# Seven-product feed-forwards of a two-layer decoder trunk: partial sums accumulated in PSUM instead of added by VectorE

## The chip, the cores and the metric

The kernel runs on one core of a Trainium2 chip. The metric is device time in microseconds, the median of several runs of the whole program. A profile of one further execution gives what each engine did and when.

## What is computed

Two layers, each a token mixer and a gated feed-forward with a convolution, every one of them between two RMS norms, on 512 tokens of 1024 features in float32. Layer 0 mixes with dilated attention, layer 1 with a gated linear recurrence. The change lies in the feed-forward of both layers:

```python
def conv_ffn(x, w_up, conv_w, conv_b, w_down):
    u = causal_dwconv(x @ w_up, conv_w, conv_b)
    g, v = u[..., :D_FF], u[..., D_FF:]
    return (jax.nn.gelu(g, approximate=True) * v) @ w_down
```

`w_up` is 1024 x 6144, `w_down` 3072 x 1024. The same seven-product scheme also serves the values of attention, where the change only turns signs.

## The kernel before, in words

**Precision.** Every operand is split into a high part `hi` (fp32r) and a rest `lo`. A product is three TensorE passes, hi·hi, hi·lo and lo·hi (`PASSES`). ScalarE makes `hi` (line 253, `whi` for weights), VectorE makes `lo` as the difference (line 265, `wlo`). Weights arrive as `raw` tiles over the Sync queue, or as `sum` tiles: one block is loaded and another added to it by a GpSimd DMA that accumulates. Up to eight split weight units are alive at once (`W_UNITS`), and `tick()`, called after every tile of the program, splits the next ones.

**Feature tiles.** The usual tile of the up projection (`feat`, line 570) is 24 matmuls of 512 columns into one PSUM bank `ps`. Then ScalarE applies the middle tap of the convolution and the bias (line 817), VectorE adds two more taps (line 821), both reading the bank, and gelu (line 831) and the gate product (line 833) follow.

**Seven products for eight.** Some pairs of blocks are multiplied as 2 x 2 block matrices with seven products instead of eight. The tokens' four corners enter directly or as *token sums* (T1 to T4, `token_sums`, line 583: VectorE adds at line 608, ScalarE takes `hi` at line 610, VectorE `lo` at line 614); the weights' sums come through the DMAs. In the *up* projection this is `sevenths` (line 840): seven products of 24 matmuls with 256 columns, for two of the six groups in `PAIRS`. Each yields one bank `vq`. Its steps are woven between feature tiles by `WIDE_STEPS = (1, 3, 1, 2)`: one product after the first tile, three after the second, one after the third, two after the fourth. In the *down* projection it is `down_unit` (line 967), two units in each feed-forward, each with seven products of 24 matmuls with 512 columns into two banks. `DOWN_AT` places each product behind a feature tile.

**What becomes of a product.** ScalarE copies the first results to SBUF (`y` and `c`, lines 869 and 872; `c` at line 990), VectorE adds or subtracts every further product from its bank (lines 873 to 887 and, through `each`, 647) and writes the outputs (`w` at line 864; `o`, `y`, `c`). Every product takes new banks from the pool of eight, oldest free one first.

**Order.** The schedule is manual: on each engine instructions run as the program wrote them. ScalarE's row for a product therefore stands behind everything that was written before it, whether that waits or not. The token sums of a feed-forward are made while its first feature tiles run, one step per `tick`.

Of the kernel before, what the change touches and what calls it, by code (L numbers as in the profile page):

```python
# [18 lines left out]
P = 128  # L19
# [76 lines left out]
def kernel(  # L96
# [485 lines left out]

    def token_sums(hT):

        made = {}
        terms_of = {
            3: [((1, 1), 1), ((0, 1), -1)],
            2: [((0, 0), 1)],
            4: [((1, 0), -1)],
            1: [((0, 1), 1), ((0, 0), -1)],  # L590
        }

        def make(pace):
            pace = iter(pace)
            prior, rest = None, []
            for name in (3, 2, 4, 1):
                hi, lo = (htp.tile([P, 4, 256], F32R, tag="x", name=nm("T"), bufs=8) for _ in range(2))
                made[name] = hi, lo
                parts = [(corner(hT, *ij)(x).bitcast(F32), sg) for ij, sg in terms_of[name] for x in range(2)]
                if name in (3, 1):  # L600
                    first = parts.pop(0)[0]
                    prior = [first[:, 2 * h : 2 * h + 2] for h in range(2)]
                r = [gen(s="run").rearrange("p (k c) -> p k c", k=2) for _ in range(2)]
                for h in range(2):
                    k = slice(2 * h, 2 * h + 2)
                    a = prior[h]
                    for b, sg in parts:
                        nc.vector.tensor_tensor(r[h], a, b[:, k], op=ALU.add if sg > 0 else ALU.subtract)  # L608
                        a = r[h]
                    nc.scalar.activation(hi[:, k], r[h], AF.Copy)  # L610
                    for f in rest:
                        f()
                    rest = [
                        lambda k=k, a=a, hi=hi, lo=lo: nc.vector.tensor_tensor(
                            lo[:, k], a, hi[:, k].bitcast(F32), op=ALU.subtract
                        )
                    ]
# [6 lines left out]
    def product(banks, act):  # L624
        i = chunk()
        while plan[i][0] == "first":
            i = chunk()
        for j in range(2):
            W = take(i, j)
            for u in range(2):  # L630
                for k in range(2):
                    for n, (a, b) in enumerate(PASSES):
                        mm(  # L633
                            banks[u],
                            act(a)[:, 2 * j + k, u * P : (u + 1) * P],
                            woven(W[b][:, k, :]),
                            start=(j, k, n) == (0, 0, 0),
                            stop=(j, k, n) == (1, 1, 2),
                        )
            done()  # L640
# [4 lines left out]
    def each(dst, a, b, op):  # L645
        for u in range(2):
            nc.vector.tensor_tensor(dst[u], a[u], b[u], op=op)

# [163 lines left out]
    def ffn(layer, hT, post, pre, spill):  # L812
# [27 lines left out]
        def sevenths(j, n):  # L840
            outs = {}

            def product(piece, act, *then):
                W = take(*piece)
                q = psum("vq")
                for n in range(2):
                    for k in range(4):
                        mm3(
                            q[:, n * 256 : (n + 1) * 256],
                            [w[:, k, n * P : (n + 1) * P] for w in W],  # L850
                            [woven(act(a)[:, k, :]) for a in range(2)],
                            k == 0,
                            k == 3,
                        )
                done()
                return q

            def out(p, s, a, q, op):
                if p not in outs:
                    outs[p] = [gen(s="w") for _ in range(2)]  # L860
                for n in range(2):
                    c = slice(n * 256, (n + 1) * 256)
                    dst = outs[p][n].rearrange("p (a b s) -> p s a b", a=2, s=2)[:, s]
                    nc.vector.tensor_tensor(dst, unwoven(a[:, c]), unwoven(q[:, c]), op=op)
# [7 lines left out]
            nc.scalar.activation(c, q, AF.Copy)  # L872
# [27 lines left out]
        def operands(base):  # L900
# [9 lines left out]
            def of(src, sign=None, prior=None):  # L910
                hi, lo = slot(), slot()
                whole = sign is not None
                if whole:
# [5 lines left out]
                    nc.scalar.activation(hi, run, AF.Copy)  # L919
# [4 lines left out]
                if whole:  # L924
                    nc.vector.tensor_tensor(lo, run, hi.bitcast(F32), op=ALU.subtract)
# [8 lines left out]
            yield of(piece(0, 0), 1)  # L934
            yield of(piece(1, 0), -1)
            yield of(piece(1, 1))
            yield of(piece(0, 0), -1, piece(0, 1))
# [29 lines left out]
        def down_unit(unit, ops):  # L967

            c, y = [gen(s="c") for _ in range(2)], [gen(s="y") for _ in range(2)]

            def step(combine):
                op = ready.pop(0)
                q = two()
                product(q, lambda a: op[a])
                begin_operand(ops)
                write()
                combine(q)
# [10 lines left out]
            def p1(q):  # L988
                for u in range(2):
                    nc.scalar.activation(c[u], q[u], AF.Copy)  # L990

            def p2(q):
                each(y, c, q, ALU.add)

            def p3(q):
                o = [gen(s="o") for _ in range(2)]
                each(o, c, q, ALU.add)
                out(0, 0, o)

            def p4(q):  # L1000
                each(y, q, y, ALU.subtract)
                each(c, q, c, ALU.subtract)

            def p5(q):
                o = [gen(s="o") for _ in range(2)]
                each(o, y, q, ALU.subtract)
                out(1, 0, o)

            def p6(q):
                each(c, q, c, ALU.subtract)  # L1010

            def p7(q):
                each(y, y, q, ALU.add)
                each(c, c, q, ALU.subtract)
                out(1, 1, y)
                out(0, 1, c)

            for p in (p1, p2, p3, p4, p5, p6, p7):
                step(p)
# [58 lines left out]
    def attention(hT, post, pre, spill):  # L1078
# [129 lines left out]
        def value_steps(out, c=None):  # L1208
# [20 lines left out]
            each(y, q, y, ALU.subtract)  # L1229
            each(c, q, c, ALU.subtract)  # L1230
# [3 lines left out]
            each(c, q, c, ALU.subtract)  # L1234
# [4 lines left out]
            each(o, y, q, ALU.subtract)  # L1239
# [4 lines left out]
            each(y, y, q, ALU.add)  # L1244
            each(c, c, q, ALU.subtract)
# [615 lines left out]
```

## Time and profile before

| | |
|---|---|
| median of 3 runs | 1375.66 us (1374.78 to 1377.14) |
| the profiled execution | 1376.62 us |
| its span, first to last instruction | 1374.9 us |
| TensorE busy | 1354.0 us, 98% |
| VectorE busy | 1052.6 us, 77% |
| ScalarE busy | 671.5 us, 49% |
| mean granted TensorE clock | 0.997 |

The engines are called PE (TensorE matmul), PEld (its weight load), DVE (VectorE), ACT (ScalarE), POOL (GpSimd) and SP (SyncE) in the profile. Rows of a timeline give start, duration, engine, line, operation, output<-input and shape; "[3.65 <-DVE run L608]" is the idle time of the engine before that row and what ended it. Matmuls are pipelined, so that the duration of one is more than the distance from one start to the next: the distance is what a matmul costs. The first feed-forward runs from about 485 to 850 us, the second from about 1003 us to the end.

### The profile page before, as it was taken

What the parts mean: (1) busy time and instruction counts of PE and PEld (TensorE: products, weight loads), DVE (VectorE), ACT (ScalarE), POOL (GpSimd) and SP (SyncE); (2) the same over time, 40 slices, a digit from 0 to 9 for tenths busy, and PEclk for the clock granted to TensorE, in tenths of its full rate; (3) what the DMA queues carried; (4) which work ended last, traced back from release to release, by engine and by line L of the source; (5) the groups of instructions that cost most, each with busy time, mean ns of one, the idle gap of its engine ahead of it and who ended that gap; (6) DMA issues with size and microseconds to landing.
All of it is one profiled execution on the core that took longest, in us unless ns stands there. A gap on an engine that the chain in (4) does not pass through costs nothing.

```text
span 1374.9 us, 18692 instructions
## 1 busy us (share of the span) xinstructions
PE 1354.0 (98%) x7109; PEld 1199.2 (87%) x7109; DVE 1052.6 (77%) x1838; ACT 671.5 (49%) x1125; POOL 111.3 (8%) x126
## 2 busy tenths in 40 slices
PE   9999999999999999999999999999999999999997
PEld 6888888888888889998888889888899998888886
DVE  7786573737676778887958789878978888968785
ACT  5434432414355554455535445579653455545452
POOL 1211021011000001000001020000001000000020
PEclk9999999999999999999999999999999999999999
DMA  8979779695749354465757784233153665768771
GB/s 256 246 218 281 193 189 250 204 215 160 254 141 307 108 154 114 147 184 122 198 155 199 214 240 159 92 123 122 62 153 105 158 165 133 191 169 213 212 201 62
DMA packets 184238, 243.11 MB, mean 177 GB/s; under 512 B 16633, under 2 KB 135937, under 8 KB 184147
## 3 DMA queue, kind: packets, MB, share of 16 engines
q1 hardware_dynamic: 151456, 184.82, 41.0%
q0 software_dynamic: 32688, 57.09, 21.5%
q8 instruction: 56, 0.92, 0.3%
q14 instruction: 36, 0.29, 0.1%
q10 hardware_dynamic: 2, 0.00, 0.0%
HBM read 218.23 MB, written 28.36 MB: 179 GB/s over the span
## 4 chain that ended last, share of the span: by engine, by line
PE 46%; DVE 32%; ACT 11%; DMA 7%; issue 3%; DVEq 0%; SPq 0%; ACTq 0%; POOLq 0%
PE ps L436 24%; PE vq L633 10%; DVE wlo L265 9%; DVE u L821 8%; PE acc L436 7%; DMA sum<-in_ffn_w_down_dram 3%; ACT whi L253 3%; ACT u L817 2%; DVE run L608 2%; DMA raw<-in_ffn_w_down_dram 1%; DVE u L833 1%; ACT u L831 1%; DVE xb L1580 1%; PE O L1465 1%; PE S L1386 1%
## 5 line engine op out<-in xcount | busy, mean ns | idle before, releaser
L436 PE MATMUL ps<-hT,whi 128*128 128x512 f32 (+1 forms) x2528 | 698.4, 362 | 0.8 <-DVE hT L499 0.6
L436 PEld LDWEIGHTS ps<-hT,whi 128*128 128x128 f32 x2528 | 459.9, 190 | 57.5 <-ACT whi L253 1.3
L436 PE MATMUL ps<-hT,wlo 128*128 128x512 f32 (+1 forms) x1264 | 456.4, 361 | 0.2 <-DVE wlo L265 0.2
L265 DVE TENSOR_TENSOR wlo<-raw,whi 128x1024 fp32r<-128x1024 f32 x233 | 280.1, 1217 | 21.7 <-ACT whi L253 21.7
L253 ACT ACTIVATE whi<-raw 128x1024 fp32r<-128x1024 f32 x233 | 239.0, 1051 | 112.9 <-DMA raw<-in_attn_w_qkv_dram 77.1
L436 PEld LDWEIGHTS ps<-hT,wlo 128*128 128x128 f32 x1264 | 240.1, 190 | 28.5 <-DVE wlo L265 0.6
L821 DVE SCALAR_TENSOR_TENSOR u<-ps,cols,u 128x511 f32<-128x511 f32 (+1 forms) x160 | 119.5, 747 | 73.5 <-ACT u L817 70.6
L253 ACT ACTIVATE whi<-sum 128x1024 fp32r<-128x1024 f32 x68 | 70.8, 1051 | 137.6 <-DMA sum<-in_attn_w_qkv_dram 71.7
L633 PE MATMUL vq<-whi,A 128*128 128x512 f32 x448 | 137.8, 379 | 0.0
L265 DVE TENSOR_TENSOR wlo<-sum,whi 128x1024 fp32r<-128x1024 f32 x68 | 82.0, 1217 | 54.2 <-ACT whi L253 54.2
L436 PE MATMUL acc<-whi,alo 128*128 128x512 f32 x256 | 97.3, 380 | 1.2 <-DVE alo L185 1.2
L436 PE MATMUL acc<-whi,ahi 128*128 128x512 f32 x256 | 98.2, 383 | 0.0
L436 PE MATMUL acc<-wlo,ahi 128*128 128x512 f32 x256 | 97.1, 379 | 0.2 <-DVE wlo L265 0.2
L633 PEld LDWEIGHTS vq<-whi,A 128*128 128x128 f32 x448 | 84.7, 189 | 12.0
L633 PE MATMUL vq<-wlo,A 128*128 128x512 f32 x224 | 85.1, 380 | 2.0 <-DVE wlo L265 2.0
L831 ACT ACTIVATE u<-u 128x512 f32<-128x512 f32 x48 | 30.3, 631 | 111.2 <-DVE u L821 111.2
L817 ACT ACTIVATE u<-ps,cols 128x512 f32<-128x512 f32 x80 | 61.0, 763 | 6.6 <-PE ps L436 6.6
L633 PE MATMUL vq<-whi,T 128*128 128x512 f32 x192 | 59.7, 382 | 0.0
L436 PEld LDWEIGHTS acc<-whi,alo 128*128 128x128 f32 x256 | 48.4, 189 | 9.1 <-DVE alo L185 2.4
L436 PEld LDWEIGHTS acc<-wlo,ahi 128*128 128x128 f32 x256 | 48.4, 189 | 7.1 <-DVE wlo L265 0.6
L436 PEld LDWEIGHTS acc<-whi,ahi 128*128 128x128 f32 x256 | 48.4, 189 | 6.6 <-ACT ahi L184 0.2
L633 PEld LDWEIGHTS vq<-wlo,A 128*128 128x128 f32 x224 | 42.3, 189 | 8.8 <-DVE wlo L265 2.9
(245 smaller groups left out, 1778.9 us busy)
## 6 DMA issues: line engine op xcount, KB each, us to landing
raw<-in_ffn_w_up_dram SPq DMA_DIRECT2D x44, 1024.0 KB
raw<-in_attn_w_qkv_dram SPq DMA_DIRECT2D x25, 1024.0 KB
raw<-in_ffn_w_down_dram SPq DMA_DIRECT2D x16, 1024.0 KB
sum<-in_ffn_w_down_dram POOLq DMA_DIRECT2D x16, 1024.0 KB, 8.7
sum<-in_attn_w_qkv_dram POOLq DMA_DIRECT2D x24, 512.0 KB, 8.1
raw<-in_attn_w_qkv_dram SPq DMA_DIRECT2D x16, 512.0 KB
sum<-in_ffn_w_down_dram SPq DMA_DIRECT2D x8, 1024.0 KB
raw<-in_lru_w_in_dram SPq DMA_DIRECT2D x8, 1024.0 KB
```

The source lines that it names most:

```text
L253: nc.scalar.activation(hi, raw, AF.Copy)
L265: nc.vector.tensor_tensor(lo, raw, hi.bitcast(F32), op=ALU.subtract)
L436: mm(dst, l[a], r[b], start=start and n == 0, stop=stop and n == 2)
L608: nc.vector.tensor_tensor(r[h], a, b[:, k], op=ALU.add if sg > 0 else ALU.subtract)
L633: mm(banks[u], act(a)[:, 2 * j + k, u * P : (u + 1) * P], woven(W[b][:, k, :]), start=(j, k, n) == (0, 0, 0), stop=(j, k, n) == (1, 1, 2),)
L817: nc.scalar.activation(u, ps, AF.Identity, scale=cc[:, j : j + 1], bias=cc[:, 48 + j : 49 + j])
L821: nc.vector.scalar_tensor_tensor(u[:, d:], ps[:, : S - d], wc, u[:, d:], op0=ALU.mult, op1=ALU.add)
L831: nc.scalar.activation(u, u, AF.Gelu_apprx_tanh)
L833: nc.vector.tensor_tensor(gv[k], gv[k], u, op=ALU.mult)
L1386: mm(ps[:, c], q[hh][:, c], keys, start=True, stop=True)
L1465: mm(po[:, c], vtile(v, r, 2 * gi + hh), pts[gi][:, r], start=gi == 0, stop=gi == 1)
L1580: nc.vector.scalar_tensor_tensor(u[:, d:], ps[:, : S - d], wc, u[:, d:], op0=ALU.mult, op1=ALU.add)
```

## The change

**Accumulation.** `product` takes a flag `first`; without it the first matmul does not clear the bank, and the product adds to what lies there. In each set of seven two chains run so: products 1 and 5 in bank W, and products 2, 4 and 7 (down) or 2, 4 and 6 (up) in bank X. The remaining ones go to a bank of their own (Z). So that all additions have the right sign, token sums 1 and 2 are negated (`flip`: ScalarE copies with scale −1, VectorE makes `lo` by one scalar_tensor_tensor).

**Copies.** `kept` has ScalarE copy a partial sum out of its bank in the middle of a chain. VectorE then adds once for each output.

**Signs elsewhere.** Attention's value steps use the same token sums; additions become subtractions, and twelve tensor_tensor operations become scalar_tensor_tensor (`less`).

The core of the diff:

```diff
+    def low(lo, whole, hi, flip=False):
+        if flip:
+            nc.vector.scalar_tensor_tensor(lo, whole, -1.0, hi.bitcast(F32), op0=ALU.mult, op1=ALU.subtract)
+        else:
+            nc.vector.tensor_tensor(lo, whole, hi.bitcast(F32), op=ALU.subtract)
+
+    def kept(bank, scale=1.0):
+        t = gen(s="c")
+        nc.scalar.activation(t, bank, AF.Copy, scale=scale)
+        return t
...
-            1: [((0, 1), 1), ((0, 0), -1)],
+            1: [((0, 0), 1), ((0, 1), -1)],
...
-                    nc.scalar.activation(hi[:, k], r[h], AF.Copy)
+                    nc.scalar.activation(hi[:, k], r[h], AF.Copy, scale=-1.0 if name == 2 else 1.0)
...
-            tt, add, sub = nc.vector.tensor_tensor, ALU.add, ALU.subtract
-            c, y = gen(s="c"), gen(s="y")
-            q = product((n + 5, 0), total_of(3))
-            nc.scalar.activation(y, q, AF.Copy)
+            add, sub = ALU.add, ALU.subtract
+            W, X = psum("W"), psum("X")
+            product(W, (n + 5, 0), total_of(3))
+            w = kept(W, -1.0)
             yield
-            q = product((n + 4, 0), corner(hT, 0, 0))
-            nc.scalar.activation(c, q, AF.Copy)
-            tt(y, y, q, op=add)
+            product(X, (n + 4, 0), corner(hT, 0, 0))
+            c = kept(X)
             yield
-            q = product((n + 4, 1), corner(hT, 1, 0))
-            out(0, 0, c, q, add)
+            Z = psum("Z")
+            product(Z, (n + 4, 1), corner(hT, 1, 0))
+            out(0, 0, c, Z, add)
             yield
-            q = product((n + 5, 1), total_of(2))
-            tt(y, q, y, op=sub)
-            tt(c, q, c, op=sub)
+            product(X, (n + 5, 1), total_of(2), False)
+            u = kept(X, -1.0)
             yield
-            q = product((n + 7, 0), total_of(4))
-            out(1, 0, y, q, sub)
+            product(W, (n + 7, 0), total_of(4), False)
+            out(1, 0, u, W, sub)
             yield
-            q = product((n + 7, 1), total_of(1))
-            out(1, 1, y, q, add)
-            tt(c, c, q, op=add)
+            product(X, (n + 7, 1), total_of(1), False)
+            out(0, 1, X)
+            out(1, 1, w, X, sub)
             yield
-            q = product((n + 8, 0), corner(hT, 1, 1))
-            out(0, 1, q, c, sub)
+            Z = psum("Z")
+            product(Z, (n + 8, 0), corner(hT, 1, 1))
+            out(0, 1, None, Z, add)
...
-            for p in (p1, p2, p3, p4, p5, p6, p7):
-                step(p)
+            def last(q):
+                o = [kept(b) for b in q]
+                made(1, 1, "w", ALU.subtract)(q)
+                each(o, o, held.pop("z"), ALU.add)
+                out(0, 1, o)
+
+            for do in (
+                (X, True, keep("c")),
+                (W, True, keep("w", -1.0)),
+                (None, True, made(0, 0, "c", ALU.add)),
+                (X, False, keep("u", -1.0)),
+                (W, False, made(1, 0, "u", ALU.subtract)),
+                (None, True, keep("z")),
+                (X, False, last),
+            ):
+                step(*do)
                 yield
```

In `down_unit`, `keep` copies both banks of a product with `kept`, and `made` lets VectorE combine a held copy with the banks into an output.

What stands where now: TensorE in the first set of `sevenths` of the first feed-forward, before. These are the first matmuls of the second product (`vq987`), the last of the third (`vq991`) and the first of the fourth (`vq996`):

```order
L436 MATMUL vq987_5067<-hT0780_3932,whi945_4814 128x256
L436 MATMUL vq987_5067<-hT1781_3933,whi945_4814 128x256
...
L436 MATMUL vq991_5105<-hT1781_3933,whi950_4855 128x256
L436 MATMUL vq991_5105<-hT0780_3932,wlo951_4856 128x256
L436 MATMUL vq996_5140<-T954_4889,whi958_4897 128x256
L436 MATMUL vq996_5140<-T955_4890,whi958_4897 128x256
```

And the same place after the change:

```order
L860 MATMUL X974_4988<-hT0780_3932,whi945_4814 128x256
L860 MATMUL X974_4988<-hT1781_3933,whi945_4814 128x256
...
L860 MATMUL Z991_5104<-hT1781_3933,whi950_4855 128x256
L860 MATMUL Z991_5104<-hT0780_3932,wlo951_4856 128x256
L860 MATMUL X974_4988<-T954_4889,whi958_4897 128x256
L860 MATMUL X974_4988<-T955_4890,whi958_4897 128x256
```

The matmuls stand in the same order; the second and the fourth product now write one bank, X, with only the third between them.

ScalarE at that place, before (`T` are token sums, `whi` weights, `u` a feature tile's convolution, `c` the copy of the second product):

```order
L817 ACTIVATE u979_5048<-ps978_5023,cols366_1819 128x512
L610 ACTIVATE T980_5052<-run982_5054 128x512
L253 ACTIVATE whi984_5061<-raw960_4901 128x1024
L872 ACTIVATE c973_4987<-vq987_5067 128x512
L610 ACTIVATE T980_5052<-run983_5055 128x512
L253 ACTIVATE whi988_5099<-sum920_4603 128x1024
L253 ACTIVATE whi994_5135<-raw986_5065 128x1024
L253 ACTIVATE whi997_5169<-sum920_4603 128x1024
```

And after:

```order
L829 ACTIVATE u979_5048<-ps978_5023,cols366_1819 128x512
L621 ACTIVATE T980_5052<-run982_5054 128x512
L253 ACTIVATE whi984_5061<-raw960_4901 128x1024
L591 ACTIVATE c987_5091<-X974_4988 128x512
L621 ACTIVATE T980_5052<-run983_5055 128x512
L253 ACTIVATE whi988_5098<-sum920_4603 128x1024
L253 ACTIVATE whi994_5134<-raw986_5065 128x1024
L591 ACTIVATE c996_5163<-X974_4988 128x512
L253 ACTIVATE whi997_5167<-sum920_4603 128x1024
```

The copy of the second product keeps its place; a copy of X after the fourth product (`c996`) is new, ahead of a weight split.

More of the change, by code (lines that the diff above doesn't have):

```diff
@@ L622, in token_sums, with product @@
         return (lambda name: lambda a: made[name][a]), make
-    def product(banks, act):
+    def product(banks, act, first=True):
         i = chunk()
@@ L636, in product @@
                             woven(W[b][:, k, :]),
-                            start=(j, k, n) == (0, 0, 0),
+                            start=first and (j, k, n) == (0, 0, 0),
                             stop=(j, k, n) == (1, 1, 2),
+                            skip_group_check=True,
                         )
@@ L647, in each, with less @@
             nc.vector.tensor_tensor(dst[u], a[u], b[u], op=op)
+    def less(dst, a, b):
+        for u in range(2):
+            nc.vector.scalar_tensor_tensor(dst[u], a[u], -1.0, b[u], op0=ALU.mult, op1=ALU.subtract)
     def feat_tiles(n, hT, sink, halves=False, between=None, at=None, paired=True):
@@ L841, in sevenths, with product, out @@
             outs = {}
-            def product(piece, act, *then):
+            def product(bank, piece, act, first=True):
                 W = take(*piece)
-                q = psum("vq")
                 for n in range(2):
                     for k in range(4):
[L848 to L854, printed above, removed]
+                        for p, (a, b) in enumerate(PASSES):
+                            mm(
+                                bank[:, n * 256 : (n + 1) * 256],
+                                W[a][:, k, n * P : (n + 1) * P],
+                                woven(act(b)[:, k, :]),
+                                start=first and (n, k, p) == (0, 0, 0),
+                                stop=(k, p) == (3, 2),
+                                skip_group_check=True,
+                            )
                 done()
-                return q
-            def out(p, s, a, q, op):
+            def out(p, s, a, q=None, op=None):
                 if p not in outs:
@@ L908, in operands, with of @@
             run = slot(F32)
-            def of(src, sign=None, prior=None):
+            def of(src, sign=None, prior=None, flip=False):
                 hi, lo = slot(), slot()
@@ L924, in of @@
                 if whole:
-                    nc.vector.tensor_tensor(lo, run, hi.bitcast(F32), op=ALU.subtract)
+                    low(lo, run, hi, flip)
                 else:
@@ L967, in down_unit, with step @@
         def down_unit(unit, ops):
-            c, y = [gen(s="c") for _ in range(2)], [gen(s="y") for _ in range(2)]
-            def step(combine):
+            W, X, held = two("W"), two("X"), {}
+            def step(banks, first, then):
                 op = ready.pop(0)
-                q = two()
-                product(q, lambda a: op[a])
+                q = banks or two()
+                product(q, lambda a: op[a], first)
                 begin_operand(ops)
                 write()
-                combine(q)
+                then(q)
                 end_operand()
@@ L986, in out, with keep, f, made @@
                         parts[t, p] = tiles[u]
[L988 to L1016, printed above, removed]
-            for p in (p1, p2, p3, p4, p5, p6, p7):
-                step(p)
+            def keep(name, scale=1.0):
+                def f(q):
+                    held[name] = [kept(b, scale) for b in q]
+                return f
+            def made(p, s, name, op):
+                def f(q):
+                    o = held.pop(name)
+                    each(o, o, q, op)
+                    out(p, s, o)
+                return f
+            def last(q):
[13 more added lines that the diff above has]
+                step(*do)
                 yield
@@ L1228, in value_steps @@
             product(q, total_of(2))
-            each(y, q, y, ALU.subtract)
-            each(c, q, c, ALU.subtract)
+            each(y, q, y, ALU.add)
+            each(c, q, c, ALU.add)
             yield
@@ L1233, in value_steps @@
             product(q, corner(hT, 1, 1))
-            each(c, q, c, ALU.subtract)
+            each(c, q, c, ALU.add)
             yield
@@ L1238, in value_steps @@
             o = [gen(s="v") for _ in range(2)]
-            each(o, y, q, ALU.subtract)
+            less(o, y, q)
             out(1, 0, o)
@@ L1243, in value_steps @@
             product(q, total_of(1))
-            each(y, y, q, ALU.add)
-            each(c, c, q, ALU.subtract)
+            less(y, y, q)
+            each(c, c, q, ALU.add)
             out(1, 1, y)
```

17 lines of the change are left out of this document (8 added, 9 removed).

## The prediction

> **What bounds the kernel now.** I read the page first, then TensorE's waits, then the order of time on TensorE and ScalarE around the seven products.
>
> ```profile
> PE 1354.0 (98%) x7109; PEld 1199.2 (87%) x7109; DVE 1052.6 (77%) x1838; ACT 671.5 (49%) x1125; POOL 111.3 (8%) x126
> PE 46%; DVE 32%; ACT 11%; DMA 7%; issue 3%; DVEq 0%; SPq 0%; ACTq 0%; POOLq 0%
> ```
>
> TensorE is busy for 1354.0 of 1374.9 us, and the change leaves it every matmul. VectorE work that is removed can therefore give back only what TensorE waits for, at most the 20.9 us in which it is idle. The second line, the chain, still runs over VectorE for 32%: in the feed-forwards TensorE runs ahead of VectorE and ScalarE, and the chain follows the laggards until TensorE once meets them. The waits say how often it does:
>
> ```profile
> PE tr L489 <- DVE xs L481: 4.0, 3, 2.6
> PE vq L633 <- DVE wlo L265: 2.0, 2, 1.2
> PE acc L436 <- DVE alo L185: 1.2, 1, 1.2
> ```
>
> The first line is the norm between two layers, which the change does not touch. The other two, 3.2 us together, lie in feed-forwards and hang on VectorE being late. They are what a lighter VectorE can win. The first of them stands behind a transfer:
>
> ```profile
> 682.75 6.65 DMA sum<-in_ffn_w_down_dram
> 690.04 12.83 DMA sum<-in_ffn_w_down_dram
> ```
>
> VectorE's splits free the sum tile at 682.7, two transfers follow, and the weights reach TensorE too late.
>
> **The new wait.** In `sevenths` (one set of seven products of the up projection, 24 matmuls of 256 columns each) the second product now goes to bank X, the third to Z, and the fourth into X again. ScalarE's copy `c` reads X after the second product, so the fourth must wait for that copy. Before, the fourth had a bank of its own. Here are the first matmuls of products two, three and four of the first set in the first feed-forward, and then ScalarE's rows up to the copy:
>
> ```profile
> 541.56 0.38 PE L436 MATMUL vq<-hT,whi 128*128 128x256 f32 x2
> ...
> 544.24 0.39 PE L436 MATMUL vq<-hT,whi 128*128 128x256 f32 x2
> ...
> 546.92 0.39 PE L436 MATMUL vq<-T,whi 128*128 128x256 f32 x2
> ```
>
> ```profile
> 553.05 0.63 ACT L610 ACTIVATE T<-run 128x512 fp32r<-128x512 f32 x1 [3.65 <-DVE run L608]
> 553.59 1.05 ACT L253 ACTIVATE whi<-raw 128x1024 fp32r<-128x1024 f32 x1
> 554.54 0.58 ACT L872 ACTIVATE c<-vq 128x512 f32<-128x512 f32 x1
> ```
>
> The second product ends as the third begins, near 544.2; the copy runs from 554.54 to 555.12, over 10 us later, because ScalarE works through a token sum (which waited for VectorE) and a weight split first. Up to this point the order shows the same instructions on both engines as before, but for the sign in two splits. So the copy comes no earlier, and the fourth product, which started at 546.92, cannot start before 555.12: 8.20 us of TensorE standing still. The second feed-forward repeats it:
>
> ```profile
> 1066.45 0.39 PE L436 MATMUL vq<-T,whi 128*128 128x256 f32 x2
> ```
>
> ```profile
> 1074.07 0.58 ACT L872 ACTIVATE c<-vq 128x512 f32<-128x512 f32 x1
> ```
>
> 1074.65 − 1066.45 is again 8.20 us. To each I add 0.05 for the handing on and 0.13 for two splits of the token sums, which lie on the chain ahead of the copy and become scalar_tensor_tensor (priced below): 8.4 us.
>
> What the standstill does to the clock is shown by TensorE's one long wait in the trace, 2.6 us at the norm ahead of the first feed-forward. These are the windows behind it, with the granted clock in the third column from the right, and then the same 48 matmuls there and, undisturbed, ahead of the second feed-forward:
>
> ```profile
> 492.00:494.00 2.00, 2.00 (x13) 1.96 (x13) 1.95 (x5) 1.23 (x3) 0.00 (x0) 0.59 1.00 323
> 494.00:496.00 2.00, 2.00 (x12) 2.00 (x12) 1.75 (x2) 2.00 (x3) 0.99 (x1) 0.55 0.55 187
> ```
>
> ```profile
> 493.33 6.60 PE ps L436 x48
> ...
> 1004.24 5.36 PE ps L436 x48
> ```
>
> The clock lost (0.41 + 0.45) × 2 = 1.72 us; the matmuls alone took 1.24 us longer. A wait of 8.4 us is three times as long, so I take the whole 1.7 us, with 0 and twice that, 3.4, as ends. The Trainium skill, "TensorE: Matmul & The Clock Gate", section "Part 1: The HAM clock gate", states half clock after an idle window of about 3.4 us and full clock after a busy one; as an estimate from that page, a resumption would cost between half a window and a whole one, 1.7 to 3.4 us. The trace agrees with one window at half clock and no run here shows two.
>
> One stall with its slow clock is 10.1 us, two are 20.2 us. No other work covers them: TensorE works in order, and behind the fourth product stand the feature tile and all later products.
>
> **The second set of each feed-forward** has the same bank order:
>
> ```profile
> 586.40 0.39 PE L436 MATMUL vq<-T,whi 128*128 128x256 f32 x2
> ...
> 1105.93 0.39 PE L436 MATMUL vq<-T,whi 128*128 128x256 f32 x2
> ```
>
> ```profile
> 588.35 0.75 ACT L817 ACTIVATE u<-ps,cols 128x512 f32<-128x512 f32 x1
> 589.06 1.06 ACT L253 ACTIVATE whi<-raw 128x1024 fp32r<-128x1024 f32 x1
> 590.03 0.58 ACT L872 ACTIVATE c<-vq 128x512 f32<-128x512 f32 x1
> ...
> 1109.46 0.58 ACT L872 ACTIVATE c<-vq 128x512 f32<-128x512 f32 x1
> ```
>
> By these rows it would stand 590.61 − 586.40 = 4.2 us, and 4.1 us in the other feed-forward. But TensorE comes 10.1 us later by then, while ScalarE's chain is hardly moved: between the sets it was held by transfers and VectorE, not by TensorE. What counts is then whether the copy fits into the third product, 24 × 0.112 = 2.7 us (544.24 to 546.92 above). The copy takes 0.58; what stands ahead of it (0.75 and 1.06) starts when the feature tile ends, a whole product earlier. So 2.1 us are to spare and I count nothing here.
>
> **The work taken off and added.** Prices by form:
>
> ```profile
> L647 DVE TENSOR_TENSOR c<-vq,c 128x512 f32<-128x512 f32 x28 | 18.0, 681 | 3.2 <-PE vq L633 3.2
> L864 DVE TENSOR_TENSOR w<-y,vq 128x256 f32<-128x256 f32 x16 | 7.0, 480 | 0.0
> L990 ACT ACTIVATE c<-vq 128x512 f32<-128x512 f32 x8 | 4.2, 577 | 0.0
> L614 DVE TENSOR_TENSOR T<-run,T 128x512 fp32r<-128x512 f32 x24 | 16.4, 682 | 0.0
> L821 DVE SCALAR_TENSOR_TENSOR u<-ps,cols,u 128x511 f32<-128x511 f32 x80 | 59.6, 746 | 70.6 <-ACT u L817 70.6
> ```
>
> A set of `sevenths` drops four 128x512 operations of VectorE and keeps its eight of 128x256; a down unit goes from 16 to 8. With four sets and four units that is 16 + 32 = 48 × 0.68 = 32.7 us off VectorE. ScalarE gets 12 copies in the sets (eight of them 128x256, no dearer than 0.58) and 32 in the units: 44 × 0.58, at most 25.5 us. The sign costs 0.746 − 0.682 = 0.064 us wherever a tensor_tensor becomes scalar_tensor_tensor: 6 token splits and 12 operations of attention's values, 1.2 us, and twice that each for four splits of 1024 columns, 0.5 us. All of this lies beside TensorE and counts nothing, but for the two splits above. What hides it is TensorE's lead, which the stalls enlarge: they give VectorE and ScalarE 10.1 us in each feed-forward. That also carries off the two waits of the table. The weights that came 1.2 us late are now wanted 10 us later, so 3.2 us are won.
>
> Other new waits: in the down units the product that goes into X or W again comes at least three feature tiles and two products after the copy, 26 us by the order (five times 24 matmuls of 0.216 us; a row for that spacing stands below), more than the 21 us of the worst lag in the rows, shown below. X and W hold four of the eight banks, so at worst a feature tile's bank is taken again after three tiles, 72 × 0.216 = 15.6 us, where it was 21 or more. ScalarE's copies stand ahead of weight splits in its queue and wait there for a product; the splits behind them, and VectorE's halves of these splits, have the same 10 us in hand. The DMAs on the Sync and GpSimd queues stand as before.
>
> **The sum.** Against the profiled execution, 1376.6 us for a span of 1374.9: + 2 × 8.4 + 2 × 1.7 − 3.2 = + 17.0, or 1393.6 us. It lies 1.0 above the median of the runs, 1375.66; on that the forecast is 1392.7 us.
>
> **The rivals.**
>
> *The lead does not last into the second set.* If VectorE and ScalarE fall back behind TensorE within the 40 us between the sets, the second set stands 4.2 us too in each feed-forward: + 8.4, 1401.1 us. For it: the lag of 10 us was built up in 50 us at the head of the feed-forward. Against it: the rows show it falling, from 10.9 to 6.9 us, already without any relief (copy's end less the end of the second product, 544.2 and 583.7, which is 2.7 us ahead of the fourth). It decides from 2.1 us of lag on.
>
> *Banks run short in the down units.* ScalarE can stand for a transfer, and a tile's bank is then not freed:
>
> ```profile
> 684.97 0.38 PE L436 MATMUL ps<-hT,wlo 128*128 128x512 f32 x1
> 685.18 0.38 PE L633 MATMUL vq<-whi,A 128*128 128x512 f32 x1
> ...
> 702.96 1.07 ACT L253 ACTIVATE whi<-sum 128x1024 fp32r<-128x1024 f32 x1 [14.28 <-DMA sum<-in_ffn_w_down_dram]
> 703.92 0.76 ACT L817 ACTIVATE u<-ps,cols 128x512 f32<-128x512 f32 x1
> ...
> 704.72 1.53 DVE L821 SCALAR_TENSOR_TENSOR u<-ps,cols,u 128x511 f32<-128x511 f32 x2 [13.46 <-ACT u L817]
> ```
>
> That tile's last matmul ended at 685.3 and its bank was free at 706.2: 21 us, and 15.6 are granted in the worst places. (The first two rows, 0.21 us apart, are also the spacing of matmuls of 512 columns.) It would cost 5.4 us in each feed-forward, 1403.5 us. Against it: here, at the sixth product, the order gives 26 us, and TensorE comes 10 us later.
>
> *The copy is in time and the change is faster.* One mechanism: ScalarE reaches `c` within the third product, 2.7 us. Then there is no stall, only the 3.2 us won: 1372.5 us. It decides at a lag of 2.1 us at the copy; the trace shows 10 us and 6 us, and nothing ahead of the copy is taken away. The Trainium skill, "PSUM — Partial Sum Buffer", section "PSUM bank collisions raise a hardware error", asks that TensorE and ScalarE be kept off one bank by semaphores; by that rule the wait cannot be loosened without another bank. No run here shows a collision.
>
> *The standstill is given back.* If TensorE's lead were mere waiting elsewhere, the time would stay, 1375.7 us. Against it stand the windows behind the first stall, of which these are the first and the last of six:
>
> ```profile
> 550.00:575.00 25.00, 25.00 (x160) 23.09 (x160) 22.30 (x31) 11.04 (x13) 0.00 (x0) 1.00 0.46 135
> ...
> 675.00:700.00 25.00, 25.00 (x117) 21.89 (x117) 16.22 (x24) 6.55 (x8) 1.28 (x1) 1.00 0.81 231
> ```
>
> TensorE works in 25.00 of 25.00 us in all six; there is nothing to give back from.
>
> **How the numbers follow.** Forecast 0.75; second set 0.12; banks 0.05; copy in time 0.05; given back 0.03. The forecast's own range: below, 8.2 us without any slow clock and also the 4.0 us of the norms won, + 9.2, 1384.9; above, 3.4 us of slow clock and no wait removed, + 23.6, 1399.3. I give 1385 to 1402, which reaches to the second-set case (1401.1) and leaves out the banks and the two on the other side, 0.13. A measurement of this kernel tells 0.2% (2.8 us) from no change: faster 0.05, same 0.03, slower 0.92.
>
> **What would show it.** TensorE's waits would list the seven products behind ScalarE's copy, 8 us once in each feed-forward, in the first set alone; the granted clock would fall to about a half behind each; the two waits of 2.0 and 1.2 us would be gone; VectorE's busy time would be 31 us less, ScalarE's 20 to 25 more. If TensorE stands in neither set, or the waits name VectorE or a feature tile's bank, the prediction is wrong.

## The result and the profile after

| | before | after |
|---|---|---|
| median | 1375.22 us (4 runs, 1374.73 to 1377.14) | 1394.38 us (4 runs, 1390.53 to 1396.08) |
| ratio | | 1.0133, 95% interval 1.0109 to 1.0156 |
| the profiled execution / its span | 1376.62 / 1374.9 us | 1394.12 / 1392.2 us |
| mean granted clock | 0.997 | 0.991 |

The change costs 1.3%. The page of after, its busy times (engine, us, share of the span, instructions) and the shares of the chain that ended last:

```profile
PE 1357.2 (97%) x7109; PEld 1204.2 (86%) x7109; DVE 1028.6 (74%) x1790; ACT 693.2 (50%) x1169; POOL 111.2 (8%) x126
PE 49%; DVE 14%; ACT 7%; issue 2%; DMA 0%; DVEq 0%; ACTq 0%
```

VectorE lost 48 instructions and 24.0 us, its share of the chain fell from 32% to 14%, and the kernel is slower all the same. TensorE has the same 7109 matmuls, yet is busy for 3.2 us more: part of them ran at a lower clock. Its waits, in us in total, times, longest:

```profile
PE X L860 <- ACT c L591: 16.2, 2, 8.1
PE tr L489 <- DVE xs L481: 3.9, 3, 2.6
```

The wait on bank X is new. The two that a lighter VectorE could win, 2.0 us on `wlo` in the down units and 1.2 us on `alo`, are gone from the list. Where the new wait stands, TensorE in the first set of the first feed-forward:

```profile
546.94 0.39 PE L860 MATMUL Z<-hT,whi 128*128 128x256 f32 x2
547.16 0.28 PE L860 MATMUL Z<-hT,wlo 128*128 128x256 f32 x1
555.52 0.80 PE L860 MATMUL X<-T,whi 128*128 128x256 f32 x2 [8.08 <-ACT c L591]
```

And ScalarE there:

```profile
553.41 0.63 ACT L621 ACTIVATE T<-run 128x512 fp32r<-128x512 f32 x1 [3.65 <-DVE run L619]
553.95 1.04 ACT L253 ACTIVATE whi<-raw 128x1024 fp32r<-128x1024 f32 x1
554.89 0.58 ACT L591 ACTIVATE c<-X 128x512 f32<-128x512 f32 x1
```

The third product (bank Z) issues its last matmul at 547.16; the fourth, into X, starts 8.36 us later, 8.24 more than the usual 0.112. It starts 0.05 us after ScalarE's copy `c` ended, and that copy stands where it stood before the change, behind a token sum and a weight split. The second feed-forward has the same at 1083.33, again 8.24 us. In the second set of the first feed-forward the same bank order costs nothing. ScalarE's copy, and the first matmul of the fourth product:

```profile
595.51 0.60 ACT L591 ACTIVATE c<-X 128x512 f32<-128x512 f32 x1 [0.95 <-PE X L860]
```

```profile
598.00 0.39 PE L860 MATMUL X<-T,whi 128*128 128x256 f32 x2
```

Here ScalarE waited 0.95 us for the product: it is no longer behind. The copy ended at 596.11, 1.9 us ahead of the matmul that needs X.

The granted clock (third column from the right) behind the two stalls, in windows of 2 us; PE's busy time is the first number after the window's length:

```profile
551.00:553.00 2.00, 0.00 (x0) 0.00 (x0) 1.93 (x4) 0.00 (x0) 0.00 (x0) 0.59 0.37 57
...
555.00:557.00 2.00, 1.48 (x7) 1.48 (x8) 1.93 (x4) 0.47 (x1) 0.00 (x0) 0.50 0.29 70
557.00:559.00 2.00, 2.00 (x11) 2.00 (x11) 2.00 (x4) 1.58 (x2) 0.00 (x0) 0.50 1.06 366
559.00:561.00 2.00, 2.00 (x11) 2.00 (x11) 2.00 (x4) 0.00 (x0) 0.00 (x0) 0.50 0.67 188
561.00:563.00 2.00, 2.00 (x10) 1.69 (x9) 0.51 (x2) 1.29 (x2) 0.00 (x0) 0.85 1.07 378
```

```profile
1083.00:1085.00 2.00, 1.67 (x8) 1.67 (x9) 1.93 (x4) 0.28 (x1) 0.00 (x0) 0.50 0.38 99
1085.00:1087.00 2.00, 2.00 (x11) 2.00 (x11) 2.00 (x4) 1.58 (x2) 0.00 (x0) 0.50 1.07 376
1087.00:1089.00 2.00, 2.00 (x14) 1.89 (x14) 2.00 (x4) 0.83 (x1) 0.00 (x0) 0.94 0.71 192
```

After the first stall TensorE lost (1.48 + 2 + 2) × 0.50 + 2 × 0.15 = 3.0 us to the clock, after the second 1.67 × 0.50 + 2 × 0.50 + 2 × 0.06 = 2.0. Two stalls and this make 16.5 + 5.0 = 21.5 us. The span grew by 17.3, so 4.2 were won: 3.2 by the two waits that are gone; 1.0 I have not placed (one execution stands against one here).

### The profile page after: what moved, and what is told of

Same layout as the page of the kernel before. It is cut to its first block, busy times and chain, and to the rows that moved or that the text cites. A ratio compares the mean times of both kernels' runs of the same rounds, so it can differ in the third digit from the quotient of the medians.

```text
span 1392.2 us, 18717 instructions
## 1 busy us (share of the span) xinstructions
PE 1357.2 (97%) x7109; PEld 1204.2 (86%) x7109; DVE 1028.6 (74%) x1790; ACT 693.2 (50%) x1169; POOL 111.2 (8%) x126
## 4 chain that ended last, share of the span: by engine, by line
PE 49%; DVE 14%; ACT 7%; issue 2%; DMA 0%; DVEq 0%; ACTq 0%
PE ps L436 25%; PE acc L436 8%; PE X L640 4%; PE W L640 3%; PE vq L640 3%; PE X L860 2%; DVE wlo L265 2%; DVE u L833 2%; ACT whi L253 2%; DVE run L619 2%; DVE xb L1593 1%; PE Z L860 1%; PE W L860 1%; ACT u L829 1%; DVE x L551 1%
## 5 line engine op out<-in xcount | busy, mean ns | idle before, releaser
L640 PE MATMUL X<-whi,A 128*128 128x512 f32 x192 | 59.0, 379 | 0.0
L311 POOL DMA_DIRECT2D sum<-in_ffn_w_down_dram x16 | 20.6, 1289 | 363.1 <-DMA sum<-in_ffn_w_down_dram 180.3
L845 DVE TENSOR_TENSOR u<-u,u 128x512 f32<-128x512 f32 x48 | 33.2, 692 | 13.2 <-ACT u L843 12.1
L860 PE MATMUL X<-T,whi 128*128 128x256 f32 x128 | 26.3, 309 | 16.2 <-ACT c L591 16.2
```

What stands on the lines that cost most here:

```text
L311: nc.gpsimd.dma_start(dst, src, accum_op=ALU.add)
L640: mm(banks[u], act(a)[:, 2 * j + k, u * P : (u + 1) * P], woven(W[b][:, k, :]), start=first and (j, k, n) == (0, 0, 0), stop=(j, k, n) == ...
L845: nc.vector.tensor_tensor(gv[k], gv[k], u, op=ALU.mult)
L860: mm(bank[:, n * 256 : (n + 1) * 256], W[a][:, k, n * P : (n + 1) * P], woven(act(b)[:, k, :]), start=first and (n, k, p) == (0, 0, 0), st ...
```

## The experiments

Nine kernels ran, in three groups, each group beside runs of before on its own chip. The medians of before were 1375.67, 1376.01 and 1376.20 us. The theory was that the whole loss is the wait on bank X and the clock behind it. The first rival was that the down units, where most of the new copies lie, cost something as well.

### Down units alone

The up projection gets a fresh bank for each product again and VectorE adds as before; the down units stay as after.

```diff
-            product(X, (n + 4, 0), corner(hT, 0, 0))
-            c = kept(X)
+            q = fresh((n + 4, 0), corner(hT, 0, 0))
+            nc.scalar.activation(c, q, AF.Copy)
+            tt(y, y, q, op=add)
...
-            product(X, (n + 5, 1), total_of(2), False)
-            u = kept(X, -1.0)
+            q = fresh((n + 5, 1), total_of(2))
+            tt(y, y, q, op=add)
+            tt(c, c, q, op=add)
```

> The down units accumulate as after; the seven products of the up projection go each to a fresh bank and VectorE adds as before (with the signs turned). Theory (the whole loss is the wait on bank X in the up projection and the slow clock behind it): no wait of TensorE on the copy c, clock 0.99 to 1.00, 1372 to 1376 us; 1372.5 if VectorE's relief in the down units alone removes the waits of 2.0 and 1.2 us, 1375.2 if that needed the lead which the standstill gave. Rival A (part of the loss lies in the down units: their banks held longer, ScalarE's 32 more copies): slower than before by 2 us or more, 1377 to 1385, with new waits on feature tiles' banks.

Measured: 1378.28 us median of 12 runs that spread from 1372.33 to 1380.44; ratio 1.0012, 0.9999 to 1.0026. No wait on a copy; the loss of after is gone, so it lay in the up projection. But nothing was won either. The time lies above the theory's range and inside rival A's, though the interval includes no change. TensorE's waits on late rests of splits:

```profile
PE ps L436 <- DVE wlo L265: 2.9, 3, 2.1
...
PE X L640 <- DVE wlo L265: 0.8, 2, 0.6
```

The 2.1 us are at 730.48, and VectorE's rows ahead of it show one part of why:

```profile
722.64 1.42 DVE L938 TENSOR_TENSOR A<-u,u 128x256 f32<-128x256 f32 x4
725.67 1.28 DVE L655 TENSOR_TENSOR c<-c,X 128x512 f32<-128x512 f32 x2 [1.61 <-ACT c L591]
726.87 1.28 DVE L655 TENSOR_TENSOR c<-c,c 128x512 f32<-128x512 f32 x2
728.08 1.22 DVE L587 TENSOR_TENSOR A<-A,A 128x1024 fp32r<-128x1024 f32 x1
729.21 1.22 DVE L265 TENSOR_TENSOR wlo<-raw,whi 128x1024 fp32r<-128x1024 f32 x1
```

In the last step of a down unit VectorE waits 1.61 us for ScalarE's copy, and the split's rest that TensorE wants next stands behind it (it ends at 730.43). So if rival A named a real cost, it was in another place: no feature tile's bank was short. Whether the copy or a late transfer sets this wait comes further down. (In the down units the chains are products 1, 4 and 7 in X and products 2 and 5 in W; the part on the change names them wrongly.)

### Up projection alone

The down units as before, the up projection as after.

```diff
-            W, X, held = two("W"), two("X"), {}
+            c, y = [gen(s="c") for _ in range(2)], [gen(s="y") for _ in range(2)]
...
+            def p4(q):
+                each(y, y, q, ALU.add)
+                each(c, c, q, ALU.add)
```

> The up projection accumulates as after; the down units take fresh banks and VectorE adds as before (with the signs turned). Theory: both waits of 8.2 us stand as in after, with 3 to 5 us of slow clock; if the lead removes the 2.0 and 1.2 us as well, 1393 to 1396 us. Rival A (part of the loss lies in the down units): 1385 to 1391. Rival B (the lead alone does not remove the two waits): 1397.

Measured: 1392.65 us (4 runs, 1391.82 to 1395.89), ratio 1.0123, 1.0103 to 1.0144.

```profile
PE X L860 <- ACT c L591: 16.2, 2, 8.1
...
PE acc L436 <- DVE wlo L265: 0.4, 1, 0.4
```

Both stalls are there (8.26 and 8.28 us from start to start), and neither the 2.0 us on `wlo` in the down units nor the 1.2 us on `alo` is left, although the down units' VectorE work is that of before. Without relief there, the lead that the stalls give is enough to remove these waits. The time lies 0.35 us below the theory's range and above rival A's.

### Work in place of the standstill

After, with matmuls that nothing uses ahead of the fourth product in the first set of each feed-forward.

```diff
+            if j == 2:
+                warm = psum("warm")
+                for _ in range(38):
+                    mm(warm, hT[0][:, 0, :P], hT[0][:, 0, :], start=True, stop=True)
             product(X, (n + 5, 1), total_of(2), False)
```

> As after, with 38 additional matmuls of 512 columns (8.2 us of work that nothing uses) into a bank of their own ahead of the fourth product in the first set of each feed-forward: TensorE computes where it stood. Theory (the clock is lost because TensorE idles, and costs about 5 us in all): no fall of the granted clock there, mean clock 0.997, 1388 to 1390 us, runs closer together than after's 5.5 us. Rival (the lower clock behind the stall is no loss of its own): 1394 us as after. If the filler is longer than the wait, its excess shows as work, not as a wait.

Measured: 1390.06 us (4 runs, 1389.94 to 1391.98), ratio 1.0101, 1.0085 to 1.0118; mean clock 0.997. TensorE at the place, and the windows there:

```profile
546.79 8.81 PE L896 MATMUL warm<-hT 128*128 128x512 f32 x38
...
555.43 0.38 PE L860 MATMUL X<-T,whi 128*128 128x256 f32 x2
```

```profile
550.00:555.00 5.00, 5.00 (x24) 4.14 (x23) 4.90 (x8) 2.07 (x3) 0.00 (x0) 1.00 0.30 48
555.00:560.00 5.00, 5.00 (x36) 4.71 (x35) 4.93 (x9) 1.64 (x3) 0.00 (x0) 1.00 0.69 220
```

The granted clock stays at 1.00, TensorE does 76 matmuls more, and the kernel is 4.3 us faster than after by the medians. The copy `c` ends at 555.00 here, 0.43 us before the fourth product starts; after had 0.05. The second feed-forward has the same 0.43. So the filler is some 0.4 us too long in each place, and the slow clock is worth about 5.1 us as an estimate from these numbers; after's windows gave 5.0. The four runs also lie closer together, 2.0 us apart instead of 5.6.

### The first two products changed round

```diff
-            product(W, (n + 5, 0), total_of(3))
-            w = kept(W, -1.0)
-            yield
             product(X, (n + 4, 0), corner(hT, 0, 0))
             c = kept(X)
             yield
+            product(W, (n + 5, 0), total_of(3))
+            w = kept(W, -1.0)
+            yield
```

The order in which the weights are split changes with them.

> As after, but the first two products of each set in the up projection change places (bank X first, then W), and their weight splits with them. A feature tile and two products then lie between the product that c copies and the one that takes X again, some 3 x 5.2 + 2 x 2.7 us instead of one product's 2.7. Theory: the copy is in time, no wait on X, clock 0.997, waits of 2.0 and 1.2 us gone: 1371 to 1374 us, faster than both kernels. Rival (TensorE would meet VectorE and ScalarE in any case after some 8 us of lag, whatever bank it is): another wait takes its place, 1385 to 1394. Rival (the copy w of bank W, now second, or the weights of the first product, now wanted earlier, stop TensorE): a wait there of 1 to 5 us each, 1376 to 1384.

Measured: 1380.56 us (12 runs, 1376.91 to 1384.01), ratio 1.0026, 1.0014 to 1.0039: 14 us faster than after, 0.26% slower than before, inside the range of the last rival. The expectation had counted the distance wrongly: one feature tile lies between the first product and the second, not three, so it is 5.2 + 2 × 2.7 = 10.6 us.

```profile
PE X L860 <- ACT c L591: 2.3, 2, 1.8
PE W L860 <- ACT c L591: 1.7, 2, 0.8
PE X L640 <- DVE wlo L265: 1.6, 2, 1.0
```

The second product's bank W now has the problem, ScalarE and then TensorE:

```profile
554.62 1.04 ACT L253 ACTIVATE whi<-raw 128x1024 fp32r<-128x1024 f32 x1
555.57 0.58 ACT L591 ACTIVATE c<-W 128x512 f32<-128x512 f32 x1
```

```profile
543.82 0.28 PE L860 MATMUL W<-T,wlo 128*128 128x256 f32 x1
...
556.20 0.49 PE L860 MATMUL W<-T,whi 128*128 128x256 f32 x2 [0.82 <-ACT c L591]
```

The product ended near 543.9 and its copy at 556.15: a lag of 12.2 us, of which a feature tile and two products cover 10.6 and a wait at X of 0.6 just before another part; the rest, 1.0, is the stall. The stalls no longer give a lead, and there are waits on split rests in the down units, all of them in the second feed-forward; those of before lay in the first.

### Products spread further, and VectorE reading the bank

The swapped kernel with another weave, the order of the weight splits moved to match, and without ScalarE's copy in the last step of a down unit.

```diff
-WIDE_STEPS = (1, 3, 1, 2)
+WIDE_STEPS = (2, 1, 2, 2)
...
-                o = [kept(b) for b in q]
                 made(1, 1, "w", ALU.subtract)(q)
-                each(o, o, held.pop("z"), ALU.add)
-                out(0, 1, o)
+                made(0, 1, "z", ALU.add)(q)
```

> As the swapped kernel, with WIDE_STEPS (2, 1, 2, 2) in place of (1, 3, 1, 2): two feature tiles and two products lie between a bank's copy and its next product, about 2 x 5.2 + 2 x 2.7 = 15.8 us against 10.6 in the swapped kernel (whose expectation named three tiles, where one lies between); the lag of ScalarE's copies there was 12 us (W: product ended 544.2, copy 556.15). In the last step of a down unit VectorE also reads the bank itself in place of ScalarE's copy. Theory: no wait on X or W in the up projection, 1373 to 1377 us. Rival (weights are wanted a tile earlier than their splits come): waits on a split's rest in the up projection of 2 us or more, 1378 to 1384.

Measured: 1389.77 us (5 runs, 1387.45 to 1390.29), ratio 1.0092, 1.0073 to 1.0112. Neither the theory nor its rival: there is no stall at the fourth and fifth product, but one at the sixth, which takes X after the copy `u` of the fourth. TensorE (the first matmuls of the fourth, fifth and sixth product), and ScalarE:

```profile
551.44 0.38 PE L860 MATMUL X<-T,whi 128*128 128x256 f32 x2
...
554.12 0.39 PE L860 MATMUL W<-T,whi 128*128 128x256 f32 x2
...
568.23 0.80 PE L860 MATMUL X<-T,whi 128*128 128x256 f32 x2 [6.09 <-ACT c L591]
```

```profile
566.64 1.06 ACT L253 ACTIVATE whi<-raw 128x1024 fp32r<-128x1024 f32 x1 [3.97 <-DMA raw<-in_ffn_w_up_dram]
567.60 0.58 ACT L591 ACTIVATE c<-X 128x512 f32<-128x512 f32 x1
```

The fourth product ended near 554.1 and its copy at 568.18, a lag of 14.1 us. The new weave left only one product and one tile there, 7.9 us, where the old one had 13.1; the difference, 6.2, is the stall. The chain in X has three products and two copies between them; I had checked the first link and the one in W. The copy stood behind a split that waited 3.97 us for its transfer. The second feed-forward stalled at the same product for 6.8 us; the split ahead of that copy had waited 2.95 us for its transfer.

### A bank of its own for the second product

After, but the second product goes to Y, the fourth opens X afresh, and VectorE adds `c`. The chain in W and the second link in X stay.

```diff
-            product(X, (n + 4, 0), corner(hT, 0, 0))
-            c = kept(X)
+            Y = psum("Y")
+            product(Y, (n + 4, 0), corner(hT, 0, 0))
+            c = kept(Y)
...
-            product(X, (n + 5, 1), total_of(2), False)
-            u = kept(X, -1.0)
+            X = psum("X")
+            product(X, (n + 5, 1), total_of(2))
+            u = gen(s="u")
+            nc.vector.scalar_tensor_tensor(u, c, -1.0, X, op0=ALU.mult, op1=ALU.subtract)
+            tt(w, w, c, op=sub)
...
-            out(0, 1, X)
+            out(0, 1, c, X, add)
```

> As after, but in the up projection the second product goes to a bank of its own (Y) and the fourth opens X afresh; VectorE adds the copy c where X lacked it (two more operations of 512 columns a set); the chain in W and the second half of the chain in X stay. Theory (not accumulating in itself, but taking X again one product after its copy was asked for, costs the 8.2 us): no wait on X, clock 0.997; but without the lead from the stalls the split weights come late in the down units as in the down-only kernel (3.7 us of waits there): 1375 to 1379 us. Rival (the chain as such stops TensorE, wherever it begins): a wait of 4 us or more stays at bank W, 1384 or more.

Measured: 1373.36 us (12 runs, 1371.15 to 1376.33), ratio 0.9977, 0.9965 to 0.9988: faster than both kernels, and faster than expected. TensorE at the place, and ScalarE:

```profile
547.74 0.28 PE L860 MATMUL Z<-hT,wlo 128*128 128x256 f32 x1
547.85 0.39 PE L860 MATMUL X<-T,whi 128*128 128x256 f32 x2
```

```profile
555.52 0.57 ACT L591 ACTIVATE c<-Y 128x512 f32<-128x512 f32 x1
```

The copy is as late as ever, 555.52, and nobody waits for it: the fourth product follows the third within 0.11 us. So the chain as such is harmless (W and the second link of X still run), and the 8.2 us belong to taking X again one product after it was to be copied. The waits on `wlo` in the down units and on `alo` are gone here too. Others stand in the list:

```profile
PE ps L436 <- DVE wlo L265: 2.3, 2, 1.7
```

Both lie ahead of the first feed-forward, where the program is that of after, which had none there. All in all TensorE stood idle for 21.3 us, before for 20.9. From the first tile of the first feed-forward (495.25, before 492.98) to the end this execution is 5.6 us shorter: 3.2 are the two waits and about 1.4 the slow clock behind the norm, which did not come in this execution; 1.0 is not placed. Ahead of that tile it is 2.3 us longer. So the 0.23% is measured by the runs, and the traces don't show which part of it the edit won.

### VectorE reading the bank in the down units

The down-only kernel with the same edit of the last step as above, and the kernel with the bank of its own with it.

> As the down-only kernel, but in the last step of a down unit VectorE adds bank X to z itself: as many VectorE operations, 8 fewer copies by ScalarE in all, and VectorE no longer waits for a copy there (1.61 us in the trace of the down-only kernel, ahead of the split whose rest TensorE wanted 2.3 us too late). Theory (the down units' own loss is this wait of VectorE): the wait of 2.3 us falls below 1, 1375 to 1377 us. Rival (the splits are late through their transfers, the wait is beside the point): 1378 as the down-only kernel.

> Both edits, the bank of its own for the second product and VectorE reading bank X in the last step of a down unit. Theory: neither wait, 1373 to 1376 us, the best of the accumulating kernels, within 0.2% of before: only the 3.2 us of waits were to be won and the transfers hold part of them. Rival (without a lead VectorE is late anyway): 1377 to 1380.

Measured: 1375.59 us (12 runs, 1371.01 to 1377.76), ratio 0.9987, 0.9973 to 1.0001, and 1373.41 us (12 runs, 1371.04 to 1378.37), ratio 0.9982, 0.9970 to 0.9994. In the first the 2.1 us on `wlo` at 730 are gone; VectorE goes through:

```profile
720.61 1.43 DVE L938 TENSOR_TENSOR A<-u,u 128x256 f32<-128x256 f32 x4
721.95 2.47 DVE L655 TENSOR_TENSOR c<-c,X 128x512 f32<-128x512 f32 x4
724.34 1.22 DVE L587 TENSOR_TENSOR A<-A,A 128x1024 fp32r<-128x1024 f32 x1
725.48 1.22 DVE L265 TENSOR_TENSOR wlo<-raw,whi 128x1024 fp32r<-128x1024 f32 x1
```

The rest is ready at 726.70 instead of 730.43. Of these 3.7 us, 1.6 are VectorE's wait for the copy; about 2 are a transfer that landed earlier, for which ScalarE waited 3.11 us just before, and 5.17 in the down-only kernel. The kernel with the bank of its own keeps the copy: its VectorE waits the same 1.61 us for it (722.42), ScalarE had waited 3.37 us for that transfer, the rest is ready at 727.18, and TensorE does not wait. So the copy alone does not make TensorE stand. In the down-only kernel with the edit a wait on `alo` near the end takes part of the win back:

```profile
PE acc L436 <- DVE alo L185: 1.6, 1, 1.6
```

The profiled execution is one of the slowest of the twelve, 1377.68 us. By the ratios the edit won 0.25% in the down-only kernel and nothing on top of the bank of its own. Since the transfer had its part, and the two ran on different chips, the copy's share of the 0.25% is not settled.

### The bank of its own, up projection alone

The kernel with the bank of its own, with the down units as before.

> The up projection as in the kernel with a bank of its own for the second product; the down units take fresh banks and VectorE adds as before (with the signs turned). It tells which half brought the 0.23% that kernel won. Theory (VectorE's relief in the down units, 32 operations, brings it, and the up projection only must not lose it): the waits of 2.0 and 1.2 us on late rests are back, 1375 to 1377 us. Rival (the up projection's order alone brings it): 1372 to 1374, without those waits.

Measured: 1374.71 us (12 runs, 1371.83 to 1378.38), ratio 0.9990, 0.9979 to 1.0002.

```profile
PE acc L436 <- DVE alo L185: 1.3, 1, 1.3
...
PE vq L640 <- DVE wlo L265: 0.8, 1, 0.8
```

The wait on `alo` is back, as the theory had it. That on `wlo` is not: the 0.8 us lie in the second feed-forward, and where before waited 2.0 us, in the first, TensorE goes through. One of the two rows in before, and the same row here:

```profile
707.44 0.48 PE L633 MATMUL vq<-wlo,A 128*128 128x512 f32 x1 [1.16 <-DVE wlo L265]
```

```profile
709.12 0.38 PE L640 MATMUL vq<-wlo,A 128*128 128x512 f32 x1
```

VectorE has as many instructions here as before, 1838. But in this execution the feed-forward's first tile starts 3.5 us later than in before (496.51), and the rest is ready at 706.05 instead of 707.38. So that wait goes without relief and without a stall. The trace is the slowest of the twelve runs (1378.38 us), and the median lies in neither expected range (theory's lower end is 1375, the rival's upper 1374). Which half brought the 0.23% is open.

## Why the prediction was right

**The bound, right.** TensorE was the bound, and VectorE's 24 us less could buy no more than what TensorE waited for. In line with it, all kernels with less VectorE work and without the long stalls lie between 0.9977 and 1.0026, and the up projection alone with a bank of its own, with as many VectorE instructions as before, lies among them at 0.9990.

**The sum, right in part by luck.** 17.0 us were forecast for the profiled execution, and its span grew by 17.3. The stalls came out 0.3 us smaller than their term, the slow clock 1.6 larger, and 1.0 us was won that no term had. The median came out at 1394.4 us, 1.7 above the forecast of 1392.7.

**The stall, right to 0.2 us.** Predicted 8.4 us each, measured 8.24. The copy's place on ScalarE decided it, as the order of both engines showed. The 0.13 us for the turned token sums did not come: their rows read

```profile
L587 DVE TENSOR_TENSOR T<-run,T 128x512 fp32r<-128x512 f32 x18 | 12.3, 685 | 0.0
L585 DVE SCALAR_TENSOR_TENSOR T<-run,T 128x512 fp32r<-128x512 f32 x6 | 4.1, 685 | 0.0
```

The sign is free. My price came from the convolution's row, an instruction of the same name that reads a bank and a column of factors.

**The slow clock, mis-sized.** Predicted 1.7 us behind each stall, from the one behind a wait of 2.6 us; measured 3.0 and 2.0, together 5.0 in place of 3.4, and about 5.1 by the experiment with work in its place. The bounds, 0 and 3.4 each, held. What failed is the step from the short wait to the long one: the clock was at half from 551 to past 561, so that some 6 us of work ran in it after the first stall and 4 after the second. The length of the wait does not fix the loss either: in the up-only kernel, by windows of 1 us, two stalls of the same length lost 2.6 and 1.5. The Trainium skill, "TensorE: Matmul & The Clock Gate", section "Part 1: The HAM clock gate", has the gate watch free-running windows of 3.4 us; as an estimate from that page a resumption loses between half a window and a whole one, 1.7 to 3.4 us, depending on where the work begins. Both losses of after lie between these ends; the 1.5 us of the up-only kernel lie a little below the lower one.

**The second sets, right.** No stall, 1.9 us to spare where 2.1 were counted. The rival that the lead would not last is refuted by the row at 595.51: ScalarE waits there for TensorE.

**The two waits, right; the reason is not the only one.** I had named the lead from the stalls as what carries them off. The up-only kernel shows that this happens without relief in the down units. But the wait of 2.0 us on `wlo` is missing in all kernels that ran, also in those without a long stall, down to the one with as much VectorE work as before. In that last one TensorE came 3.0 us later than before and the rest was ready 1.3 us earlier. The wait on `alo` is there in before, in the kernel with a bank of its own in the up projection alone (1.3 us), and in the down-only kernel where VectorE reads the bank (1.6); the others don't have it.

**The down units, right for this kernel alone.** No feature tile's bank ran short. But I had priced ScalarE's copies there at nothing, with only their own queue in view; VectorE's wait of 1.61 us for a copy in the last step stands in the traces of all kernels that keep it. In the down-only kernel, with a late transfer ahead of it, TensorE met it; in after it did not.

**The rivals on the other side.** "The copy is in time" was priced at 1372.5 us. No kernel made the copy earlier; the bank of its own removed the need for it, and gave 1373.4. The price was close, which is no evidence for its reasoning: in that trace TensorE stood idle as long as before, and the part of the two waits in the win is not separated from the clock and from noise. "Given back" is refuted by the chain of numbers above: 17.3 of 21.5 us stayed.

**VectorE's busy time** fell by 24.0 us, where I had 31. The instruction count is the 48 that I had; rows of neighbours overlap, so that durations add up to more than busy time: the durations of all rows fell by 29.0. It did not enter the sum.

## What to carry to other kernels

Adding in PSUM saves the vector engine work but ties the next product to the reader of the last partial sum: for every link of the chain, compare the work that lies between the product and the bank's next use with the lag of the reader's queue, not with the copy's 0.58 us. Here stall was lag less distance each time: 10.9 − 2.7 in after, 12.2 − 10.6 − 0.6 in the swapped kernel, 14.1 − 7.9 in the spread one. Where a link is too short, break it there with one more bank and let the chain begin later: that kept 32 of the 48 saved operations and turned + 1.3% into − 0.23%. The win is that small because TensorE was busy for 98% of the time before.

## What the hardware showed that was not expected

A scalar_tensor_tensor with a constant and two SBUF operands took as long as a tensor_tensor: 685 ns each at 128x512, 1224 each at 128x1024.

After standstills of 8.2 us the granted clock stayed at half for 6 us of work in one feed-forward and 4 in the other, in the same execution; 38 matmuls without a use in each place (8.6 us from the first of them to the start of the fourth product) kept it at 1.00 and made the kernel 4.3 us faster.

After the wait at the norm, 2.60 or 2.61 us in every trace, the granted clock fell to 0.55 in before and 0.50 in after (the window from 494 to 496). In the up-only kernel, the swapped one and the one with a bank of its own it stayed at 1.00 in every window of 2 us there.
